# Nineteen more tiles are transposed on VectorE in blocks of 32 by 32, in a two-block model of 256 tokens

## The chip, the cores and the metric

The kernel runs on one core of one Trainium2 chip, in one launch. The metric is device time in microseconds, the median of several runs. A core has TensorE (PE, matmuls and transposes through the systolic array), VectorE (DVE), ScalarE (ACT), GpSimd (POOL) and SyncE (SP, which here issues the loads of weights). Each engine works through its own queue of instructions strictly in order. Data lie in on-chip buffers of 128 partitions; results of PE go to PSUM banks, from which the other engines read them.

## The reference

A first block on x (256 tokens, 2048 channels): RMS norm, one projection, three kinds of attention (gated linear, forgetting, memory), gates, an output projection, and an MLP with squared ReLU. A second block on its result: RMS norm, a projection, sparse attention beside a pool mixer, a gated sum of the two branches, memory cross-attention, and a SwiGLU. Cut to the lines whose results the change touches:

```python
xn = rms_norm(h, attn_norm_g)
gq, gk, gv, gg, ga, fq, fk, fv, fg, ff, mq, mg = split(xn @ w_in)
fq_h, fk_h = rms_norm(heads(fq), g1), rms_norm(heads(fk), g2)   # normed streams, as mk and mq
o = rms_norm(concat([gla_o, fox_o, mem_o]), out_norm_g)
gate = concat([silu(gg), sigmoid(fg), sigmoid(mg)])
h = h + (o * gate) @ w_out
u = relu(rms_norm(h, mlp_norm_g) @ w_up)
h = h + (u * u) @ w_down
# block 2, x = h
z = rms_norm(x, ln_mix_pre) @ w_in_2
a, p = nsa_attention(...), pool_mixer(...)
y = (g_a * (a @ w_br_attn) + g_p * (p @ w_br_pool)) @ w_mix_out
```

All of it is float32.

## The kernel before

**Matmuls.** Every product with a weight matrix is a group: 512 output columns for 256 tokens, summed over 16 k-tiles of 128 rows (8 for the groups called dn, ba and bp). To keep float32 accuracy with PE's faster type, both factors are split in a high and a low part. For each k-tile and each half of the tokens PE runs three matmuls of 128 by 512: high by high (line 460), high by weight-low (461), low by weight-high (462). A group of 16 k-tiles has 96 of them, one of 8 k-tiles has 48.

**Weights.** They arrive by DMA in units of two k-tiles (512 KB) into five raw buffers. For each unit ACT copies out the high part `wh` (line 133, called from `split`) and DVE subtracts to get the low part `wl` (line 366). There are six pairs of `wh` and `wl`, and up to four units are split ahead of the one that PE works on.

**Activations.** The factor that is not a weight must stand transposed, channels on partitions. A tile is 256 tokens by 512 channels: eight squares of 128 by 128, and four k-tiles once it is transposed, that is 24 matmuls of a group. There are two ways. `T_group` (under `T_split` and `T_plain`) transposes on PE against an identity: two quads of four squares, each into a PSUM bank (line 203), from which ACT writes the high part and DVE the low part. `T_dve` transposes on DVE: 16 instructions (line 525) that each turn eight blocks of 32 by 32, from buffer to buffer; then ACT and DVE split as before. Before the change `T_dve` serves the 16 u tiles of the MLP and 11 tiles of the SwiGLU, 27 tiles with 432 such instructions; all other tiles go over PE.

**Order.** The order of the instructions on each engine is fixed when the kernel is built. `run_groups` writes the matmuls of all groups in order. What has to be done with a group's result (scales, norms, gates, transposes) is a task, a generator that yields between small steps. `pump` runs between k-tiles and puts steps of waiting tasks into the queues as long as counters of estimated time (`pe_t`, `act_t`, `dve_t`) stay within LIM of each other; `dv` prices a DVE instruction. When a group's matmuls come to a k-tile whose transposed tile has no finished task yet, `need` calls `finish`, which writes the steps of all waiting tasks at once, ahead of the next matmul. SP issues the loads in the order of the units.

**Names.** The groups follow each other as mk, mv, gq, gk, sm, gv0, gv1, mq, fq, fk, fv, gg0, gg1, fg, mg, out0 to out3, up and dn in turn (dn7_0 to dn7_3 are the last four of the MLP), kvc and q0 and others of block 2's projection, m0 to m7, bp0 to bp3, ba0 to ba3, mix0 to mix3, xk, xv, xo, fg0.0 and so on. dn7_c adds into the stream x at columns c, and `norm_T` of it makes the transposed tile c that kvc needs first (16 k-tiles, tile 0 for k-tiles 0 to 3, up to tile 3). ba_c completes the branch sum y of columns c in `br`, which mix0 needs in the same manner. In the orders, s and a number are activation buffers, gb the banks of groups, pb the banks of transposes and attention, vecs the norms' gains.

Of the kernel before, what the change touches and what calls it, by code (L numbers as in the profile page):

```python
# [10 lines left out]
F32 = mybir.dt.float32  # L11
# [3 lines left out]
OP = mybir.AluOpType  # L15
# [93 lines left out]
class Program:  # L109
# [405 lines left out]

        yield from self.T_group(nat, sink)

    def T_dve(self, f, hi, lo):

        (g,) = yield from self.F.wait()  # L520
        x = f.rearrange("p (t k q j) -> p k t q j", t=2, k=4, q=4)
        y = g.rearrange("p (k t a i) -> p k t a i", k=4, t=2, a=4)
        for a in range(4):
            for q in range(4):
                self.nc.vector.transpose(y[32 * q:32 * q + 32, :, :, a], x[32 * a:32 * a + 32, :, :, q])  # L525
                self.dv(256)
                if q % 2:
                    yield 1
        self.F.put(f)
        self.act(hi, g)  # L530
        yield 1
        self.tt(lo, g, hi.bitcast(F32), OP.subtract)
        self.F.put(g)

    def T_plain(self, nat, dst, gain=None):
# [69 lines left out]
def v3(f, a):  # L605
    return f.rearrange("p (a b) -> p a b", a=a)


class Kernel(Program):
# [57 lines left out]
    def headnorm_T(self, banks, key, gain, name):  # L667
        yield from self.until(("rs", key))
        rs = self.rs[key]
        f, j = yield from self.F.wait(2)  # L670
        for t in range(2):
            self.scopy(v3(f, 2)[:, t], banks[t], rs[:, t:t + 1])
        yield "B"
        self.act(j, f, AF.Square)
        yield 1
        ss = self.stat(8)
        self.red(ss, v3(j, 8), OP.add)
        self.F.put(j)
        r = self.rstd(ss, 8, 128.0)
        yield 1  # L680
        self.tt(v3(f, 8), v3(f, 8), r[:, :, None].to_broadcast([128, 8, 128]), OP.mult)
        yield 1
        (o,) = yield from self.F.wait()
        yield from self.T_plain(v3(f, 2), o, gain)
        self.F.put(f)
        self.S[name] = o
        self.ev.add(name)

    def plain_T(self, banks, key, scale, name, keep=False):
        yield from self.until(("rs", key))  # L690
        rs = self.rs[key]
        if scale != 1.0:
            r2 = self.stat(2)
            self.ts(r2, rs, scale)
            rs = r2
        f, o = yield from self.F.wait(2)
        for t in range(2):
            self.scopy(v3(f, 2)[:, t], banks[t], rs[:, t:t + 1])
        yield "B"
        yield from self.T_plain(v3(f, 2), o)  # L700
        if keep:
            self.S["nat", name] = f
        else:
            self.F.put(f)
        self.S[name] = o
        self.ev.add(name)
# [316 lines left out]
    def gate(self, banks, grp, silu):  # L1023
        rs = self.rs["x"]
        (s,) = yield from self.F.wait()
        s3 = v3(s, 2)
        for t in range(2):
            self.act(s3[:, t], banks[t], AF.Sigmoid, scale=rs[:, t:t + 1])
            if silu:
                self.stt(s3[:, t], banks[t], rs[:, t:t + 1], s3[:, t], OP.mult, OP.mult)  # L1030
        if grp == 3:
            self.free_TT("x")
        yield "B"
        yield from self.until(("o", grp))
        o = self.S.pop(("o", grp))
        self.tt(o, o, s, OP.mult)
        self.F.put(s)
        yield 1
        h, l = yield from self.R.wait(2)
        yield from self.T_split(v3(o, 2), self.vec("out_norm_g", 4 * grp, 4), h, l)  # L1040
        self.F.put(o)
        self.TT["o"][0][grp], self.TT["o"][1][grp] = h, l
        self.ev.add(("oT", grp))

# [4 lines left out]
    def norm_T(self, f, c, key, gain, sq):  # L1049

        f3 = v3(f, 2)
        self.sq_into(f3, sq, c)
        self.nsq[key] = self.nsq.get(key, 0) + 1
        if self.nsq[key] == 4:
            self.fin_ssq(sq, key)
        yield 1
        h, l = yield from self.R.wait(2)
        yield from self.T_split(f3, self.vec(gain, 4 * c, 4), h, l)
        H, L = self.TT.setdefault(key, ([None] * 4, [None] * 4))
        H[c], L[c] = h, l  # L1060
        self.ev.add((key, c))
# [392 lines left out]

    def a_T(self, f, x):
        h, l = yield from self.R.wait(2)
        yield from self.T_split(v3(f, 2), None, h, l)
        self.F.put(f)
        self.TT["a"][0].append(h)
        self.TT["a"][1].append(l)  # L1460
        self.ev.add(("a", x))
# [72 lines left out]
    def br(self, banks, i, c):  # L1534

        m = 4 * i + c
        yield from self.until(("m", m))
        s = self.S["m", m]
        s3 = v3(s, 2)
        self.act(s, s, AF.Sigmoid)  # L1540
        for t in range(2):
            self.tt(s3[:, t], banks[t], s3[:, t], OP.mult)
        if c == 3:
            self.free_TT("p" if i else "a")
        yield "B"
        if i == 1:
            self.ev.add(("yp", c))
            return
        y = self.S.pop(("m", c))
        p = self.S.pop(("m", 4 + c))  # L1550
        self.tt(y, y, p, OP.add)
        self.F.put(p)
        yield 1
        h, l = yield from self.R.wait(2)
        yield from self.T_split(v3(y, 2), None, h, l)
        self.F.put(y)
        H, L = self.TT.setdefault("y", ([None] * 4, [None] * 4))
        H[c], L[c] = h, l
        self.ev.add(("y", c))
# [599 lines left out]
```

## Time and profile before

| | |
|---|---|
| median of three runs | 2617.18 us (2617.09 to 2617.91) |
| the profiled execution | 2616.85 us, of which the span is 2615.1 us |
| mean granted clock of PE | 0.998 |
| PE busy | 2591.0 us, 99% of the span |
| DVE busy | 1670.6 us, 64% |
| ACT busy | 1264.2 us, 48% |
| DVE instructions of block transposes | 432 |
| PE matmuls on line 203, transposes among them | 484 |

The span is from the first to the last instruction on the chip; the run's own time is 1.75 us longer. An engine that is busy for nearly the whole span, with the chain of waits running along it, sets the time. The other engines matter where it waits for them. Start times in the profile place the groups: out1 begins at 404.4 us, up2 at 516.9, dn7_2 at 1151.1, dn7_3 at 1162.9, kvc at 1174.7, ba3 at 1669.4, mix0 at 1681.2, mix1 at 1703.9.

### The profile page before, as it was taken

What the parts mean: (1) busy time and instruction counts of PE and PEld (TensorE: products, weight loads), DVE (VectorE), ACT (ScalarE), POOL (GpSimd) and SP (SyncE); (2) the same over time, 40 slices, a digit from 0 to 9 for tenths busy, and PEclk for the clock granted to TensorE, in tenths of its full rate; (3) what the DMA queues carried; (4) which work ended last, traced back from release to release, by engine and by line L of the source; (5) the groups of instructions that cost most, each with busy time, mean ns of one, the idle gap of its engine ahead of it and who ended that gap; (6) DMA issues with size and microseconds to landing.
All of it is one profiled execution on the core that took longest, in us unless ns stands there. A gap on an engine that the chain in (4) does not pass through costs nothing.

```text
span 2615.1 us, 31982 instructions
## 1 busy us (share of the span) xinstructions
PE 2591.0 (99%) x11980; PEld 2148.5 (82%) x11980; DVE 1670.6 (64%) x2310; ACT 1264.2 (48%) x1697; POOL 76.6 (3%) x97
## 2 busy tenths in 40 slices
PE   9999999999999999999999999999999999999998
PEld 7888888888888888888888888888788888888886
DVE  6567655686677567755566445666766656565656
ACT  7544544544444444444465444465554444444443
POOL 0001000000000000001000000000000000000001
PEclk9999999999999999999999999999999999999999
DMA  9543465555566556565444557555455555555653
GB/s 346 206 138 121 156 222 186 185 193 195 193 204 229 193 194 233 190 209 195 152 139 150 190 177 258 203 197 188 139 186 191 197 190 199 189 198 188 215 188 129
DMA packets 138892, 500.19 MB, mean 191 GB/s; under 512 B 15649, under 2 KB 16593, under 8 KB 138736
## 3 DMA queue, kind: packets, MB, share of 16 engines
q1 hardware_dynamic: 131760, 473.16, 53.4%
q0 software_dynamic: 6976, 24.98, 2.8%
q8 instruction: 94, 1.54, 0.2%
q14 instruction: 62, 0.51, 0.1%
HBM read 493.33 MB, written 7.88 MB: 192 GB/s over the span
## 4 chain that ended last, share of the span: by engine, by line
PE 94%; issue 4%; DVE 1%; ACT 0%; DMA 0%; POOL 0%; SPq 0%; DVEq 0%; ACTq 0%; POOLq 0%
PE gb L460 29%; PE gb L462 29%; PE gb L461 29%; PE pb L197 4%; PE pb L203 2%; DVE s L169 0%; DVE wl L366 0%; DMA s<-memT 0%; DVE s L158 0%; ACT wh L133 0%; POOL st L232 0%; PE gb L450 0%; ACT s L133 0%; PE gb L452 0%; PE gb L451 0%
## 5 line engine op out<-in xcount | busy, mean ns | idle before, releaser
L366 DVE TENSOR_TENSOR wl<-raw,wh 128x1024 fp32r<-128x1024 f32 (+1 forms) x876 | 1057.8, 1219 | 572.2 <-ACT wh L133 565.5
L460 PE MATMUL gb<-wh,s 128*128 128x512 f32 x3496 | 1380.0, 395 | 2.0 <-ACT wh L133 1.8
L461 PE MATMUL gb<-wl,s 128*128 128x512 f32 x3496 | 1363.3, 390 | 2.5 <-DVE wl L366 2.5
L462 PE MATMUL gb<-wh,s 128*128 128x512 f32 x3496 | 1363.6, 390 | 0.3 <-DVE s L169 0.3
L133 ACT ACTIVATE wh<-raw 128x1024 fp32r<-128x1024 f32 (+1 forms) x878 | 916.3, 1055 | 809.2 <-PE gb L462 765.1
L460 PEld LDWEIGHTS gb<-wh,s 128*128 128x128 f32 x3496 | 657.5, 188 | 138.4 <-ACT wh L133 3.4
L462 PEld LDWEIGHTS gb<-wh,s 128*128 128x128 f32 x3496 | 656.9, 188 | 138.8 <-DVE s L169 1.0
L461 PEld LDWEIGHTS gb<-wl,s 128*128 128x128 f32 x3496 | 657.7, 188 | 136.3 <-DVE wl L366 3.8
L525 DVE STREAM_TRANSPOSE s<-s 32x256 f32<-32x256 f32 x432 | 188.2, 436 | 7.8
L158 DVE TENSOR_TENSOR s<-gb,s 128x512 f32<-128x512 f32 x144 | 97.6, 690 | 124.6 <-PE gb L462 94.5
L133 ACT ACTIVATE s<-gb,st 128x512 f32<-128x512 f32 (+1 forms) x112 | 70.0, 642 | 177.4 <-PE gb L462 166.0
L133 ACT ACTIVATE s<-s 128x1024 fp32r<-128x1024 f32 (+3 forms) x89 | 82.5, 928 | 90.0 <-DVE s L525 68.5
L197 PE MATMUL pb<-s,s 128*128 128x128 f32 (+4 forms) x720 | 116.5, 301 | 1.3 <-DVE s L158 0.9
L197 PEld LDWEIGHTS pb<-s,s 128*128 128x128 f32 x720 | 97.7, 191 | 9.5 <-DVE s L158 1.3
L133 ACT ACTIVATE s<-pb 128x512 f32<-128x512 f32 (+4 forms) x117 | 56.9, 506 | 73.9 <-PE pb L203 49.7
L203 PE MATMUL pb<-cc,s 128*128 128x128 f32 (+1 forms) x484 | 73.2, 274 | 5.6 <-DVE s L169 5.6
L203 PEld LDWEIGHTS pb<-cc,s 128*128 128x128 f32 (+1 forms) x484 | 59.7, 141 | 22.4 <-DVE s L169 6.9
L158 DVE TENSOR_TENSOR s<-s,s 128x60 f32<-128x60 f32 (+5 forms) x123 | 73.8, 633 | 0.6
L133 ACT ACTIVATE s<-pb,vecs 128x256 fp32r<-128x256 f32 (+2 forms) x109 | 42.2, 453 | 50.0 <-PE pb L203 40.5
L163 DVE TENSOR_SCALAR s<-gb,st 128x512 f32<-128x512 f32 (+1 forms) x32 | 20.9, 658 | 67.8 <-PE gb L462 51.5
L169 DVE SCALAR_TENSOR_TENSOR s<-pb,vecs,s 128x256 fp32r<-128x256 f32 (+1 forms) x104 | 40.0, 435 | 29.0 <-ACT s L133 29.0
L133 ACT ACTIVATE s<-s,st 128x128 f32<-128x128 f32 (+2 forms) x73 | 32.8, 450 | 31.7 <-DVE st L163 30.4
(113 smaller groups left out, 550.7 us busy)
## 6 DMA issues: line engine op xcount, KB each, us to landing
raw<-w_in SPq DMA_DIRECT2D x216, 512.0 KB, 4.2
raw<-w_up SPq DMA_DIRECT2D x216, 512.0 KB, 4.4
raw<-w_down SPq DMA_DIRECT2D x216, 512.0 KB, 4.6
raw<-w_gate SPq DMA_DIRECT2D x88, 512.0 KB, 4.7
raw<-w_out SPq DMA_DIRECT2D x32, 512.0 KB, 4.5
raw<-w_mix_out SPq DMA_DIRECT2D x32, 512.0 KB, 4.7
raw<-w_br_pool SPq DMA_DIRECT2D x16, 512.0 KB, 5.2
raw<-w_br_attn SPq DMA_DIRECT2D x16, 512.0 KB, 4.5
```

The source lines that it names most:

```text
L133: self.nc.scalar.activation(out, in_, func, **kw)
L158: self.nc.vector.tensor_tensor(out, a, b, op)
L163: self.nc.vector.tensor_scalar(out, a, s1, None, op0=op0)
L169: self.nc.vector.scalar_tensor_tensor(out, a, s, b, op0, op1)
L197: self.nc.tensor.matmul(out, lhsT, rhs, start=start, stop=stop)
L203: self.nc.tensor.transpose(out, in_, self.ident[:k, :k])
L366: self.nc.vector.tensor_sub(l[:, :m], r, h[:, :m].bitcast(F32))
L460: mm(o, H[:, c:c + 128], wh, start=st, stop=False)
L461: mm(o, H[:, c:c + 128], wl, start=False, stop=False)
L462: mm(o, L[:, c:c + 128], wh, start=False, stop=sp)
L525: self.nc.vector.transpose(y[32 * q:32 * q + 32, :, :, a], x[32 * a:32 * a + 32, :, :, q])
```

## The change

Nineteen tiles that went over PE go through DVE's block transpose: the normed keys and queries mk, mq, fq, fk (`headnorm_T`), gq and gk (`plain_T` with `keep`), three of the four gated outputs (`gate`), columns 0 to 2 of the streams after attention and after the MLP (`norm_T` with key h and h2, three each), the first half of the sparse attention's result (`a_T`), and columns 0 to 2 of the branch sum (`br`). The sixteen instructions are taken out of `T_dve` into `T_blocks`; `T_dve` can apply a gain while splitting, and keep its source. The high and low parts are then made from the transposed tile in a buffer instead of from PSUM banks.

```diff
--- before.py
+++ after.py
@@ -515,9 +515,8 @@
 
         yield from self.T_group(nat, sink)
 
-    def T_dve(self, f, hi, lo):
-
-        (g,) = yield from self.F.wait()
+    def T_blocks(self, f, g):
+
         x = f.rearrange("p (t k q j) -> p k t q j", t=2, k=4, q=4)
         y = g.rearrange("p (k t a i) -> p k t a i", k=4, t=2, a=4)
         for a in range(4):
@@ -526,10 +525,19 @@
                 self.dv(256)
                 if q % 2:
                     yield 1
-        self.F.put(f)
-        self.act(hi, g)
-        yield 1
-        self.tt(lo, g, hi.bitcast(F32), OP.subtract)
+
+    def T_dve(self, f, hi, lo, gain=None, keep=False):
+        (g,) = yield from self.F.wait()
+        yield from self.T_blocks(f, g)
+        if not keep:
+            self.F.put(f)
+        if gain is None:
+            self.act(hi, g)
+            yield 1
+            self.tt(lo, g, hi.bitcast(F32), OP.subtract)
+        else:
+            self.split_T(v3(g, 4), gain, v3(hi, 4), v3(lo, 4))
+            yield 1
         self.F.put(g)
 
     def T_plain(self, nat, dst, gain=None):
@@ -681,8 +689,9 @@
         self.tt(v3(f, 8), v3(f, 8), r[:, :, None].to_broadcast([128, 8, 128]), OP.mult)
         yield 1
         (o,) = yield from self.F.wait()
-        yield from self.T_plain(v3(f, 2), o, gain)
+        yield from self.T_blocks(f, o)
         self.F.put(f)
+        self.scopy(o, o, gain)
         self.S[name] = o
         self.ev.add(name)
 
@@ -697,7 +706,10 @@
         for t in range(2):
             self.scopy(v3(f, 2)[:, t], banks[t], rs[:, t:t + 1])
         yield "B"
-        yield from self.T_plain(v3(f, 2), o)
+        if keep:
+            yield from self.T_blocks(f, o)
+        else:
+            yield from self.T_plain(v3(f, 2), o)
         if keep:
             self.S["nat", name] = f
         else:
@@ -1037,8 +1049,11 @@
         self.F.put(s)
         yield 1
         h, l = yield from self.R.wait(2)
-        yield from self.T_split(v3(o, 2), self.vec("out_norm_g", 4 * grp, 4), h, l)
-        self.F.put(o)
+        if grp < 3:
+            yield from self.T_dve(o, h, l, self.vec("out_norm_g", 4 * grp, 4))
+        else:
+            yield from self.T_split(v3(o, 2), self.vec("out_norm_g", 4 * grp, 4), h, l)
+            self.F.put(o)
         self.TT["o"][0][grp], self.TT["o"][1][grp] = h, l
         self.ev.add(("oT", grp))
 
@@ -1055,7 +1070,10 @@
             self.fin_ssq(sq, key)
         yield 1
         h, l = yield from self.R.wait(2)
-        yield from self.T_split(f3, self.vec(gain, 4 * c, 4), h, l)
+        if key != "hx" and c < 3:
+            yield from self.T_dve(f, h, l, self.vec(gain, 4 * c, 4), True)
+        else:
+            yield from self.T_split(f3, self.vec(gain, 4 * c, 4), h, l)
         H, L = self.TT.setdefault(key, ([None] * 4, [None] * 4))
         H[c], L[c] = h, l
         self.ev.add((key, c))
@@ -1454,8 +1472,11 @@
 
     def a_T(self, f, x):
         h, l = yield from self.R.wait(2)
-        yield from self.T_split(v3(f, 2), None, h, l)
-        self.F.put(f)
+        if x == 0:
+            yield from self.T_dve(f, h, l)
+        else:
+            yield from self.T_split(v3(f, 2), None, h, l)
+            self.F.put(f)
         self.TT["a"][0].append(h)
         self.TT["a"][1].append(l)
         self.ev.add(("a", x))
@@ -1552,8 +1573,11 @@
         self.F.put(p)
         yield 1
         h, l = yield from self.R.wait(2)
-        yield from self.T_split(v3(y, 2), None, h, l)
-        self.F.put(y)
+        if c < 3:
+            yield from self.T_dve(y, h, l)
+        else:
+            yield from self.T_split(v3(y, 2), None, h, l)
+            self.F.put(y)
         H, L = self.TT.setdefault("y", ([None] * 4, [None] * 4))
         H[c], L[c] = h, l
         self.ev.add(("y", c))
```

The order of the queues changes with it, since `T_blocks` yields eight times a tile, and since the tasks' estimated times differ. Three places follow.

PE where kvc begins, before. The tile s23 with its low part s15 is transposed tile 0; s27 is the stream's columns 3, and wh2 is the second unit of kvc:

```order
L460 MATMUL gb2_84<-wh2_74,s23_186_7449 128x512
L461 MATMUL gb2_84<-wl2_75,s23_186_7449 128x512
L462 MATMUL gb2_84<-wh2_74,s15_187_7450 128x512
L460 MATMUL gb3_85<-wh2_74,s23_186_7449 128x512
L461 MATMUL gb3_85<-wl2_75,s23_186_7449 128x512
L462 MATMUL gb3_85<-wh2_74,s15_187_7450 128x512
L203 MATMUL pb0_86<-cc_92,s27_104_2695 128x128 x4
L460 MATMUL gb2_84<-wh3_76,s11_188_7544 128x512
L461 MATMUL gb2_84<-wl3_77,s11_188_7544 128x512
L462 MATMUL gb2_84<-wh3_76,s30_189_7545 128x512
```

PE in the same place now, from the end of dn7_3. Here s5 and s10 are the high and low part of tile 0, s24 the stream's columns 3:

```order
L460 MATMUL gb1_83<-wh0_70,s16_183_7200 128x512
L461 MATMUL gb1_83<-wl0_71,s16_183_7200 128x512
L462 MATMUL gb1_83<-wh0_70,s8_184_7201 128x512
L203 MATMUL pb0_86<-cc_92,s24_107_2754 128x128 x4
L460 MATMUL gb2_84<-wh1_72,s5_192_7543 128x512
L461 MATMUL gb2_84<-wl1_73,s5_192_7543 128x512
L462 MATMUL gb2_84<-wh1_72,s10_193_7544 128x512
L460 MATMUL gb3_85<-wh1_72,s5_192_7543 128x512
L461 MATMUL gb3_85<-wl1_73,s5_192_7543 128x512
L462 MATMUL gb3_85<-wh1_72,s10_193_7544 128x512
L203 MATMUL pb1_87<-cc_92,s24_107_2754 128x128 x4
```

The first quad of tile 3 stood behind the 24 matmuls of tile 0; it now stands ahead of the first one, and that quad needs the last sum of dn7_3.

DVE from the sum of dn7_2 (s18) to that of dn7_3 (s27), before:

```order
L158 TENSOR_TENSOR s18_103_2693<-gb2_84,s18_103_2693 128x512
L158 TENSOR_TENSOR s18_103_2693<-gb3_85,s18_103_2693 128x512
L366 TENSOR_TENSOR wl1_73<-raw3_68,wh1_72 128x1024
L366 TENSOR_TENSOR wl2_75<-raw4_69,wh2_74 128x1024
L169 SCALAR_TENSOR_TENSOR s10_191_7622<-pb3_89,vecs_91,s14_190_7621 128x256 x2
L366 TENSOR_TENSOR wl3_77<-raw0_65,wh3_76 128x1024
L169 SCALAR_TENSOR_TENSOR s10_191_7622<-pb2_88,vecs_91,s14_190_7621 128x256 x2
L366 TENSOR_TENSOR wl4_79<-raw1_66,wh4_78 128x1024
L158 TENSOR_TENSOR s27_104_2695<-gb0_82,s27_104_2695 128x512
L158 TENSOR_TENSOR s27_104_2695<-gb1_83,s27_104_2695 128x512
```

DVE in the last part of the same stretch now; s21 is the stream's columns 2, and s27, s12 and s15 are tiles 0, 1 and 2 while they are being transposed. Of the sixteen transposes since the sum of dn7_2 (s21), the first four stand ahead of these rows:

```order
L366 TENSOR_TENSOR wl1_73<-raw3_68,wh1_72 128x1024
L366 TENSOR_TENSOR wl2_75<-raw4_69,wh2_74 128x1024
L524 STREAM_TRANSPOSE s15_200_7703<-s21_106_2752 32x8x32 x2
L524 STREAM_TRANSPOSE s12_197_7632<-s19_105_2750 32x8x32 x2
L524 STREAM_TRANSPOSE s27_194_7545<-s3_104_2748 32x8x32 x2
L366 TENSOR_TENSOR wl3_77<-raw0_65,wh3_76 128x1024
L524 STREAM_TRANSPOSE s15_200_7703<-s21_106_2752 32x8x32 x2
L524 STREAM_TRANSPOSE s12_197_7632<-s19_105_2750 32x8x32 x2
L366 TENSOR_TENSOR wl4_79<-raw1_66,wh4_78 128x1024
L524 STREAM_TRANSPOSE s27_194_7545<-s3_104_2748 32x8x32 x2
L158 TENSOR_TENSOR s24_107_2754<-gb0_82,s24_107_2754 128x512
L158 TENSOR_TENSOR s24_107_2754<-gb1_83,s24_107_2754 128x512
```

Between the two sums stood four weight splits and four instructions of a quarter of a tile each; there are four weight splits and sixteen block transposes now.

DVE from the sum of ba2 (s21) to the rows that follow on ba3, before; s7 is the tile of columns 3:

```order
L158 TENSOR_TENSOR s21_250_10426<-gb2_84,s21_250_10426 128x512
L158 TENSOR_TENSOR s21_250_10426<-gb3_85,s21_250_10426 128x512
L366 TENSOR_TENSOR wl4_79<-raw1_66,wh4_78 128x1024
L158 TENSOR_TENSOR s21_250_10426<-s21_250_10426,s19_233_9479 128x1024
L366 TENSOR_TENSOR wl5_81<-raw2_67,wh5_80 128x1024
L366 TENSOR_TENSOR wl0_71<-raw3_68,wh0_70 128x1024
L158 TENSOR_TENSOR s12_258_11057<-pb2_88,s27_257_11056 128x512
L158 TENSOR_TENSOR s12_258_11057<-pb3_89,s27_257_11056 128x512
L366 TENSOR_TENSOR wl1_73<-raw4_69,wh1_72 128x1024
```

DVE in that place now, up to the finished sum of columns 3 (s19). The sum of ba2 was s31, and s23, s21 and s5 are tiles 0, 1 and 2 of y on their way:

```order
L524 STREAM_TRANSPOSE s21_269_11119<-s26_259_10432 32x8x32 x2
L524 STREAM_TRANSPOSE s23_266_11033<-s20_258_10309 32x8x32 x2
L366 TENSOR_TENSOR wl0_71<-raw3_68,wh0_70 128x1024
L524 STREAM_TRANSPOSE s5_272_11204<-s31_260_10555 32x8x32 x2
L366 TENSOR_TENSOR wl1_73<-raw4_69,wh1_72 128x1024
L524 STREAM_TRANSPOSE s21_269_11119<-s26_259_10432 32x8x32 x2
L158 TENSOR_TENSOR s19_261_10678<-gb0_82,s19_261_10678 128x512
L158 TENSOR_TENSOR s19_261_10678<-gb1_83,s19_261_10678 128x512
L366 TENSOR_TENSOR wl2_75<-raw0_65,wh2_74 128x1024
L158 TENSOR_TENSOR s19_261_10678<-s19_261_10678,s16_246_9868 128x1024
L524 STREAM_TRANSPOSE s5_272_11204<-s31_260_10555 32x8x32 x2
L524 STREAM_TRANSPOSE s21_269_11119<-s26_259_10432 32x8x32 x2
```

Twelve block transposes and five weight splits stand between the products of ba2 and the finished sum of columns 3; of tile 0's low part nothing is made yet at the end of these rows.

## Rows read from the trace of the kernel before

**Rows 1.** The page: busy time by engine, the clock, the chain by engine.
```profile
PE 2591.0 (99%) x11980; PEld 2148.5 (82%) x11980; DVE 1670.6 (64%) x2310; ACT 1264.2 (48%) x1697; POOL 76.6 (3%) x97
PEclk9999999999999999999999999999999999999999
PE 94%; issue 4%; DVE 1%; ACT 0%; DMA 0%; POOL 0%; SPq 0%; DVEq 0%; ACTq 0%; POOLq 0%
```

**Rows 2.** Timeline of PE in out1: start us, duration us, engine, line, names, count.
```profile
408.23 0.39 PE L462 MATMUL gb<-wh,s 128*128 128x512 f32 x1
408.46 0.60 PE L203 MATMUL pb<-cc,s 128*128 128x128 f32 x4
408.81 0.48 PE L460 MATMUL gb<-wh,s 128*128 128x512 f32 x1
409.13 0.40 PE L461 MATMUL gb<-wl,s 128*128 128x512 f32 x1
```

**Rows 3.** Busy time by stretch: us, PE, PEld, DVE, ACT, POOL, PEclk, DMA share, GB/s.
```profile
404.40:427.10 22.70, 22.70 (x106) 18.82 (x105) 12.66 (x15) 11.28 (x16) 0.00 (x0) 1.00 0.57 182
516.90:538.70 21.80, 21.80 (x98) 18.04 (x97) 17.74 (x25) 11.46 (x13) 0.00 (x0) 1.00 0.58 194
...
1162.90:1174.70 11.80, 11.80 (x58) 9.78 (x57) 7.73 (x11) 7.04 (x12) 0.53 (x1) 1.00 0.74 237
1174.70:1197.40 22.70, 22.70 (x106) 18.81 (x105) 12.50 (x16) 10.64 (x16) 4.28 (x6) 1.00 0.89 313
...
1669.40:1681.20 11.80, 11.80 (x57) 9.80 (x56) 8.43 (x10) 6.16 (x7) 0.00 (x0) 1.00 0.53 179
1681.20:1703.90 22.70, 22.70 (x105) 18.81 (x105) 9.21 (x10) 5.66 (x7) 2.10 (x4) 1.00 0.66 231
1703.90:1727.70 23.80, 22.38 (x98) 17.95 (x97) 20.47 (x29) 18.56 (x32) 0.00 (x0) 1.00 0.66 221
224.90:258.70 33.80, 33.80 (x199) 29.65 (x198) 28.00 (x48) 13.28 (x22) 3.27 (x2) 1.00 0.33 110
```

**Rows 4.** Costliest groups of the page: busy us, mean ns of one, idle before.
```profile
L133 ACT ACTIVATE wh<-raw 128x1024 fp32r<-128x1024 f32 (+1 forms) x878 | 916.3, 1055 | 809.2 <-PE gb L462 765.1
...
L525 DVE STREAM_TRANSPOSE s<-s 32x256 f32<-32x256 f32 x432 | 188.2, 436 | 7.8
...
L203 PE MATMUL pb<-cc,s 128*128 128x128 f32 (+1 forms) x484 | 73.2, 274 | 5.6 <-DVE s L169 5.6
```

**Rows 5.** Timeline of DVE in up1, where a u tile is transposed.
```profile
509.31 1.22 DVE L366 TENSOR_TENSOR wl<-raw,wh 128x1024 fp32r<-128x1024 f32 x1
510.56 1.80 DVE L525 STREAM_TRANSPOSE s<-s 32x256 f32<-32x256 f32 x4
512.39 1.23 DVE L366 TENSOR_TENSOR wl<-raw,wh 128x1024 fp32r<-128x1024 f32 x1
513.53 1.22 DVE L158 TENSOR_TENSOR s<-s,s 128x1024 fp32r<-128x1024 f32 x1
```

**Rows 6.** Timeline of DVE around dn7_3 and kvc.
```profile
1170.56 0.87 DVE L169 SCALAR_TENSOR_TENSOR s<-pb,vecs,s 128x256 fp32r<-128x256 f32 x2
...
1174.21 1.37 DVE L158 TENSOR_TENSOR s<-gb,s 128x512 f32<-128x512 f32 x2 [1.65 <-PE gb L462]
```

**Rows 7.** Timeline of DVE around ba3, mix0 and mix1.
```profile
1669.01 1.30 DVE L158 TENSOR_TENSOR s<-gb,s 128x512 f32<-128x512 f32 x2 [0.70 <-ACT wh L133]
1670.23 1.22 DVE L366 TENSOR_TENSOR wl<-raw,wh 128x1024 fp32r<-128x1024 f32 x1
...
1704.18 1.43 DVE L158 TENSOR_TENSOR s<-gb,s 128x512 f32<-128x512 f32 x2 [11.09 <-ACT junk L133]
```

**Rows 8.** Timeline of PE in fg0.0, at an idle time of 4.43 us.
```profile
1887.53 1.46 PE L203 MATMUL pb<-cc,s 128*128 128x128 f32 x8 [4.43 <-DVE s L169]
...
1891.56 0.41 PE L462 MATMUL gb<-wh,s 128*128 128x512 f32 x1
```

**Rows 9.** Busy time by stretch, the 5 us around the end of that idle time.
```profile
1887.00:1892.00 5.00, 4.18 (x16) 3.09 (x17) 5.00 (x12) 2.17 (x8) 1.60 (x1) 0.66 0.44 168
```


## The prediction

> **What bounds the kernel now.** I read the page's busy times first, then the chain, then the stretches group by group, and last the queues of single engines. TensorE is busy for 99% of the span, its clock stays at the full level in all forty slices, and 94% of the chain runs along it [rows 1]. So time is saved only by what is taken off TensorE's queue, and lost only by what makes it wait. VectorE has 36% of the span free on average [rows 1], but the average hides how it is spread. In the groups of 16 k-tiles between which u tiles are transposed, VectorE works 17.74 of 21.80 us; in fk, beside attention, 28.00 of 33.80; in dn7_3 7.73 of 11.80 and in ba3 8.43 of 11.80 [rows 3]. The last two are the short groups: there the next matrix, which needs the fresh tiles, begins after half the time.
>
> **What leaves TensorE.** Nineteen tiles of two quads are 38 quads, 152 transposes of 128 by 128. In out1 a quad stands between two matmuls: the next matmul starts 0.35 us after the quad did, and the one behind it 0.32 us later instead of the usual 0.23, which is the distance from the matmul ahead to the quad [rows 2]. A quad thus costs 0.35 + 0.09 = 0.44 us, and 38 cost 16.7 us. A second view agrees: out1, with one tile's transposes, lasts 22.70 us, up2 without any 21.80 [rows 3]; 19 times 0.90 is 17.1. I take 16.7.
>
> **What comes to VectorE.** Nineteen times 16 is 304 block transposes of 0.44 us [rows 4], 0.45 with the gap behind each, against some 16 copies and subtractions that go: about 132 us in all, so 1.80 ms or 69% of the span. One tile takes 16 × 0.45 = 7.2 us of VectorE for 0.88 us of TensorE.
>
> Here a rule of the Trainium skill can be set beside the rows. The trace has 0.44 us for four squares on TensorE [rows 2], and for eight squares 16 block transposes of 0.44 us, 7.0 us [rows 4]. The page "VectorE: DVE Perf Modes" (The three transpose paths) gives 390 ns on TensorE and 311 ns on VectorE for one square of bf16, in 32 by 32 blocks only, and its rules for kernel authors say to transpose 128 by 128 on TensorE where a result in PSUM will do. By its figures a tile would cost VectorE about 2.5 us (an estimate: 8 × 311 ns), and the stalls below would largely vanish, which is the second case below; the trace has nearly three times that. Its advice, TensorE, speaks against this change.
>
> **Where VectorE has the room.** In long groups a tile that becomes free is needed a whole group later. mk to fk, the gated outputs and the h tiles fall into out0 to up0 and before: 12 to 18 us of other work in 21.8 [rows 3] plus 7.2 us of transposes at most once a group. I count 19 to 20 of 21.8 us in out1 to up0; in gk and fk up to 2 us more than the group has, which four units of weights split ahead (10.9 us of matmuls) absorb. I take 0 there, with 0 to 4 us as bounds. The reloaded branch tile (one more goes to DRAM and back) lies on queues that wait for nothing near; ACT, at 48% [rows 1], takes a few more table loads beside TensorE; both are taken as nothing.
>
> **Where it has not: dn7_3 to kvc.** I walk the new queue from the end of dn7_2's last matmul, with durations from the rows: a weight split 1.14 us, or 1.25 ahead of a transpose; four transposes 1.83; a sum of two halves 1.22 (1.33 ahead of a transpose); a tile-wide subtraction 1.14; a low part of a quarter tile 0.44 [rows 5 to 7]. On VectorE: sum of dn7_2 1.3, sixteen transposes 7.2, four weight splits 4.9, sum of dn7_3 1.3: done at 14.7 us. TensorE has dn7_3's 48 matmuls, 48 × 0.227 = 10.9 us, and then, in the new order, a quad of columns 3 ahead of kvc's first matmul. It waits 14.75 − 10.9 = 3.9 us. (Before, VectorE was idle for 1.65 us ahead of this sum, waiting for TensorE [rows 6].) Next, the first low part of tile 0 stands behind a weight split, two small reductions and four transposes: 14.75 + 1.1 + 0.4 + 1.8 + 0.45 = 18.5; TensorE comes at 15.6 and waits 3.0. Tile 0's 24 matmuls and the second quad end at 24.0. Before the first low part of tile 1 VectorE still does three low parts of tile 0, four of tile 3, twelve transposes and two weight splits: 1.3 + 1.75 + 5.4 + 2.3, and 0.45 for that part itself: 11.2 us, at 29.7. TensorE comes at 24.5 and waits 5.2. Tile 2's first low part is there at 34.6, TensorE comes at 35.1. In all 12.0 us. The stretch has 34 block transposes, 15.3 us: VectorE has 39.3 us of work in 33.5 us of matmuls.
>
> **ba3 to mix0** works the same way. Between the products of ba2 and the finished sum of columns 3 stand sum 1.3, twelve transposes 5.4, five weight splits 6.0, and sums and products of 3.6: it is done at 16.4 us, TensorE comes for its quad at 10.9 and waits 5.5. Behind it come eight transposes and the subtraction for tile 0's low part (3.7 + 1.2): 21.25, against 17.3 for TensorE, 3.95. Tile 0 ends at 26.7. Tile 1's last transpose is at 29.6, its high part, a copy of 1.05 us on ACT [rows 4], at 30.65: 3.95. Its low part is at 34.25, against 31.1: 3.15. Tile 2's low part stands behind a weight split whose pair of buffers TensorE frees late, at 41.85, against 39.7: 2.15. In all 18.7 us; VectorE has 42.5 us of work in 33.5.
>
> **Clock and mix1.** After an idle time of 4.43 us in fg0.0 the next eight transposes take 1.46 us instead of twice 0.6, and the granted clock is 0.66 over those 5 us, so for a while the lower level, 1.2 GHz [rows 2, 8, 9]: 0.34 × 5.0 = 1.7 us of matmul time. Each stretch above has such waits; the first slow spell hides in the wait after it, the last does not: 2 × 1.7 = 3.4 us, with 0 and 7 as bounds. In the other direction, mix1 has 2.0 us more than a group of its kind: ACT's squares of mix0's result stood ahead of the weight copies, and VectorE was idle for 11.09 us [rows 3, 7]. In the new order three more units are split ahead of them, so that goes: −2.0.
>
> **Sum.** From the profiled execution, 2616.85 us (0.33 below the median): −16.7 + 12.0 + 18.7 + 3.4 − 2.0 = +15.4, 2632.2. I predict 2632 us.
>
> **The rivals.** *Two shorter stalls, or one:* the walk charges every wait in full; if one stretch stalls as worked out and the other for a third, 2616.85 − 16.7 − 2.0 + 12 + 6 + 1 to 3 is 2617 to 2619. For it: the tasks were priced to fit. Against: rows and order leave no slack in the sums of 14.7 and 16.4 us. *The blocks are absorbed:* VectorE has 944 us free and receives 132, and transposes u tiles in up2 with no idle time on TensorE (21.80 busy of 21.80) [rows 1, 3]. Then −16.7 and −2.0 plus a few us of waits: 2598 to 2608, faster. The mechanism would be a block transpose that costs much less between weight splits than in the rows; the point is at dn7_3, where the sixteen would have to fit in 10.9 − 7.5 = 3.4 us, 0.21 us each. The rows with four in 1.83 us [rows 5] speak against it. *Attention stalls too:* fk has 5.8 us free on VectorE [rows 3] and receives a tile of 7.2 less the copies it loses; the same near mq, fq and m6. With 2 to 4 us there and the clock at the lower level more often, 2640 to 2650.
>
> **How the numbers follow.** Forecast, both stretches stall (2623 to 2640): 0.66. Shorter stalls (2612 to 2622): 0.14. Absorbed (2598 to 2611): 0.11. Attention too (above 2640): 0.09. A measurement of this kernel tells 0.2%, 5.2 us, from no change, so faster is below 2612, slower above 2622.4: 0.11, 0.14 and 0.75. The range takes in most of the second and part of the fourth: 2614 to 2643.
>
> **What would show it.** Right: line 203 has 332 instructions instead of 484, the block transposes number 736 at 0.44 us; out1 to out3 last 21.8 us; TensorE has waits released by VectorE of 4, 3 and 5 us from kvc's first quad on, and of 5.5, 4, 4, 3 and 2 in mix0, and a granted clock below 1 in both; kvc ends 12 us and mix0 19 us later against the groups ahead; mix1 is 21.8 long. Wrong: no wait above 2 us at either place, or waits of that size in mq to fk or in m0 to m7, or a block transpose of less than 0.3 us.

## The result, and the profile after

The changed kernel takes 2637.38 us (median of 4 runs, 2636.42 to 2638.48) against 2617.55 us for the kernel before (4 runs, 2617.09 to 2619.88): a ratio of 1.0073, with a 95% interval of 1.0062 to 1.0085. It is 20 us slower; 2632 us had been predicted, 15 us slower, in a range of 2614 to 2643.

The page of the changed kernel, busy times, clock, chain by engine, and the two groups of transposes:

```profile
PE 2588.6 (98%) x11828; PEld 2142.0 (81%) x11828; DVE 1795.6 (68%) x2602; ACT 1269.7 (48%) x1695; POOL 79.5 (3%) x99
PEclk9999999999999999989999999899999999999999
PE 91%; issue 5%; DVE 3%; DMA 1%; ACT 0%; POOL 0%; SPq 0%; DVEq 0%; ACTq 0%; POOLq 0%
...
L524 DVE STREAM_TRANSPOSE s<-s 32x256 f32<-32x256 f32 x736 | 320.7, 436 | 13.7 <-ACT s L133 0.5
...
L203 PE MATMUL pb<-cc,s 128*128 128x128 f32 (+1 forms) x332 | 53.4, 285 | 14.4 <-DVE s L158 9.1
```

Against [rows 1] and [rows 4] VectorE has 125 us more to do and 304 block transposes more, at the same 436 ns each; line 203 lost 152 instructions, 19.8 us of TensorE's busy time. The digits of TensorE's clock have two 8s (slices below 90% of full speed), where there were only 9s, and the chain now spends 3% on VectorE.

Busy times by stretch (us; PE, PEld, DVE, ACT and POOL busy; granted clock; DMA share; GB/s), for dn7_3, kvc, ba3, mix0, mix1 and out1 of the changed kernel:

```profile
1150.90:1167.90 17.00, 12.35 (x54) 9.52 (x52) 16.55 (x29) 7.41 (x14) 0.00 (x0) 0.96 0.51 173
1167.90:1200.10 32.20, 27.61 (x100) 21.44 (x101) 22.99 (x41) 13.58 (x23) 5.87 (x9) 0.81 0.75 261
1669.30:1686.00 16.70, 11.81 (x54) 9.60 (x52) 16.33 (x25) 6.14 (x6) 0.00 (x0) 0.98 0.52 177
1686.00:1726.90 40.90, 30.25 (x103) 23.05 (x102) 25.45 (x41) 13.98 (x21) 2.11 (x4) 0.76 0.42 147
1726.90:1748.70 21.80, 21.80 (x98) 18.08 (x97) 14.00 (x18) 12.87 (x22) 0.00 (x0) 1.00 0.59 188
396.90:418.60 21.70, 21.70 (x97) 18.00 (x96) 19.40 (x31) 11.44 (x16) 0.00 (x0) 1.00 0.54 184
```

In [rows 3] the same six were 11.80, 22.70, 11.80, 22.70, 23.80 and 22.70 us long. out1 loses its 0.9 us (0.94 by the start times of the groups, 22.70 and 21.76 us), mix1 its 2.0. The first two grow by 14.7 us together, ba3 and mix0 by 23.1. VectorE is busy for 39.5 of 49.2 and 41.8 of 57.6 us there. The groups ahead of dn7_3 are 11.9 us shorter together, those between the two places 2.8.

TensorE's waits at kvc's start and then at mix0's start in the changed kernel (start, duration, line, names, count, in brackets the idle time ahead and what ended it):

```profile
1165.89 0.33 PE L203 MATMUL pb<-cc,s 128*128 128x128 f32 x1 [3.91 <-DVE s L158]
...
1167.86 0.79 PE L460 MATMUL gb<-wh,s 128*128 128x512 f32 x1 [0.47 <-ACT s L133]
...
1170.22 0.80 PE L462 MATMUL gb<-wh,s 128*128 128x512 f32 x1 [1.15 <-DVE s L169]
...
1178.50 0.50 PE L460 MATMUL gb<-wh,s 128*128 128x512 f32 x1 [1.11 <-ACT s L133]
...
1181.57 0.80 PE L462 MATMUL gb<-wh,s 128*128 128x512 f32 x1 [2.33 <-DVE s L169]
...
1685.23 1.08 PE L203 MATMUL pb<-cc,s 128*128 128x128 f32 x4 [4.89 <-DVE s L158]
...
1690.09 0.80 PE L462 MATMUL gb<-wh,s 128*128 128x512 f32 x1 [2.93 <-DVE s L158]
...
1700.96 0.51 PE L460 MATMUL gb<-wh,s 128*128 128x512 f32 x1 [2.57 <-ACT s L133]
...
1704.66 0.80 PE L462 MATMUL gb<-wh,s 128*128 128x512 f32 x1 [2.97 <-DVE s L158]
...
1714.69 0.50 PE L462 MATMUL gb<-wh,s 128*128 128x512 f32 x1 [2.19 <-DVE s L158]
```

The first of each list is the quad of columns 3 that stands ahead of the first matmul. Line 462 needs the low part, line 460 the high part of the next tile. Each wait is released by VectorE, or by ACT right behind it. The quad's place itself matters little by these rows: behind it TensorE waits for tile 0's low part anyway, until 1170.22 and 1690.09.

VectorE's queue at the places that the prediction timed, first dn7_3 and kvc, then ba3 and mix0:

```profile
1151.78 1.28 DVE L158 TENSOR_TENSOR s<-gb,s 128x512 f32<-128x512 f32 x2
...
1165.14 1.29 DVE L158 TENSOR_TENSOR s<-gb,s 128x512 f32<-128x512 f32 x2
...
1169.68 1.67 DVE L169 SCALAR_TENSOR_TENSOR s<-s,vecs,s 128x256 fp32r<-128x256 f32 x4
...
1181.03 1.67 DVE L169 SCALAR_TENSOR_TENSOR s<-s,vecs,s 128x256 fp32r<-128x256 f32 x4
...
1187.33 1.23 DVE L366 TENSOR_TENSOR wl<-raw,wh 128x1024 fp32r<-128x1024 f32 x1 [2.45 <-ACT wh L133]
...
1668.89 1.30 DVE L158 TENSOR_TENSOR s<-gb,s 128x512 f32<-128x512 f32 x2
...
1683.95 1.22 DVE L158 TENSOR_TENSOR s<-s,s 128x1024 f32<-128x1024 f32 x1
...
1688.81 1.23 DVE L158 TENSOR_TENSOR s<-s,s 128x1024 fp32r<-128x1024 f32 x1
...
1696.76 1.23 DVE L366 TENSOR_TENSOR wl<-raw,wh 128x1024 fp32r<-128x1024 f32 x1 [1.49 <-ACT wh L133]
...
1703.38 1.23 DVE L158 TENSOR_TENSOR s<-s,s 128x1024 fp32r<-128x1024 f32 x1
...
1710.47 1.23 DVE L366 TENSOR_TENSOR wl<-raw,wh 128x1024 fp32r<-128x1024 f32 x1 [4.73 <-ACT wh L133]
...
1713.42 1.22 DVE L158 TENSOR_TENSOR s<-s,s 128x1024 fp32r<-128x1024 f32 x1
```

From the sum of dn7_2 (start at 1151.78), that of dn7_3 ends 14.65 us later, the first low part of tile 0 18.3, of tile 1 29.7 us later; 14.7, 18.5 and 29.7 were worked out. From the sum of ba2 (start at 1668.89), the finished columns 3 come 16.3 us later (walked: 16.4) and the low part of tile 0 21.15 (21.25), but that of tile 1 35.7 (34.25) and of tile 2 45.75 (41.85). In between VectorE has idle times that ACT's weight copies end: 2.45 us in kvc, behind which no wait of TensorE follows, and 1.49 and 4.73 in mix0. The walk had such a late copy only ahead of tile 2, and a shorter one. A copy waits until TensorE is done with the pair of buffers, and TensorE was slow: in five microseconds of mix0 the changed kernel's stretch reads

```profile
1690.00:1695.00 5.00, 4.91 (x14) 3.94 (x15) 4.89 (x10) 0.60 (x1) 0.53 (x1) 0.50 0.08 13
```

with a granted clock of 0.50, the lower level of 1.2 GHz.

### The profile page after: what moved, and what is told of

Same layout as the page of the kernel before. It is cut to its first block, busy times and chain, and to the rows that moved or that the text cites. A ratio compares the mean times of both kernels' runs of the same rounds, so it can differ in the third digit from the quotient of the medians.

```text
span 2636.7 us, 31964 instructions
## 1 busy us (share of the span) xinstructions
PE 2588.6 (98%) x11828; PEld 2142.0 (81%) x11828; DVE 1795.6 (68%) x2602; ACT 1269.7 (48%) x1695; POOL 79.5 (3%) x99
## 4 chain that ended last, share of the span: by engine, by line
PE 91%; issue 5%; DVE 3%; DMA 1%; ACT 0%; POOL 0%; SPq 0%; DVEq 0%; ACTq 0%; POOLq 0%
PE gb L460 28%; PE gb L462 28%; PE gb L461 28%; PE pb L197 4%; DVE s L524 1%; PE pb L203 1%; DVE wl L366 1%; DVE s L158 1%; DVE s L169 1%; DMA s<-memT 0%; DMA raw<-w_down 0%; ACT wh L133 0%; POOL st L232 0%; PE gb L450 0%; PE gb L452 0%
## 5 line engine op out<-in xcount | busy, mean ns | idle before, releaser
L524 DVE STREAM_TRANSPOSE s<-s 32x256 f32<-32x256 f32 x736 | 320.7, 436 | 13.7 <-ACT s L133 0.5
L133 ACT ACTIVATE s<-pb 128x512 f32<-128x512 f32 (+4 forms) x107 | 51.3, 499 | 71.1 <-PE pb L203 47.7
L158 DVE TENSOR_TENSOR s<-s,s 128x1024 fp32r<-128x1024 f32 (+5 forms) x127 | 78.6, 651 | 0.7
L203 PE MATMUL pb<-cc,s 128*128 128x128 f32 (+1 forms) x332 | 53.4, 285 | 14.4 <-DVE s L158 9.1
L203 PEld LDWEIGHTS pb<-cc,s 128*128 128x128 f32 (+1 forms) x332 | 42.9, 147 | 27.9 <-DVE s L158 10.5
L163 DVE TENSOR_SCALAR s<-gb,st 128x512 f32<-128x512 f32 (+1 forms) x28 | 17.9, 645 | 53.2 <-PE gb L462 37.0
L232 POOL TENSOR_TENSOR st<-st,nhalf 128x8 f32<-128x8 f32 (+2 forms) x21 | 27.9, 1331 | 799.9 <-DVE st L165 799.9
L133 ACT ACTIVATE s<-s,vecs 128x256 fp32r<-128x256 f32 (+1 forms) x87 | 39.5, 519 | 16.9 <-DVE s L524 13.0
```

Of the source, the lines that this page charges most:

```text
L133: self.nc.scalar.activation(out, in_, func, **kw)
L158: self.nc.vector.tensor_tensor(out, a, b, op)
L163: self.nc.vector.tensor_scalar(out, a, s1, None, op0=op0)
L203: self.nc.tensor.transpose(out, in_, self.ident[:k, :k])
L232: self.nc.gpsimd.tensor_tensor(r, t, self.nhalf[:, :k], op=OP.pow)
```

## The experiments

Each edit is against the changed kernel.

**Six tiles back (both_back).**

```diff
-        if key != "hx" and c < 3:
+        if key != "hx" and c < (3 if key == "h" else 0):
...
-        if c < 3:
+        if c < 0:
```

> The six tiles at the two short-group boundaries (columns 0 to 2 of the stream after the MLP, and of the branch sum) go over TensorE again; the other 13 new tiles stay on VectorE. Theory: the loss sits in these two places alone, so from the changed kernel the 14.6 us by which dn7_3 and kvc grew (less 1.6 gained in dn7_1 and dn7_2), the 23.0 us of ba3 and mix0 (less 1.9 gained in ba1 and ba2) and the 2.0 us gained at mix1 are taken back: 2637.4 - 13.0 - 19.2 = 2605, faster than before by 12. Rival (a fuller VectorE costs time in many places): the gain of 13 tiles is lost elsewhere, 2615 or more.

Measured: 2605.64 us (2604.89 to 2606.99), 0.9954 of the kernel before (0.9939 to 0.9969). dn7_3, kvc, ba3 and mix0 of this kernel:

```profile
1152.30:1164.10 11.80, 11.80 (x58) 9.78 (x56) 7.73 (x11) 7.04 (x12) 0.53 (x1) 1.00 0.76 232
1164.10:1186.80 22.70, 22.70 (x106) 18.81 (x104) 12.51 (x16) 10.65 (x16) 4.28 (x6) 1.00 0.88 315
1657.90:1669.70 11.80, 11.80 (x58) 9.78 (x56) 8.43 (x10) 6.16 (x7) 0.00 (x0) 1.00 0.53 179
1669.70:1692.40 22.70, 22.70 (x106) 18.81 (x104) 9.17 (x10) 5.70 (x7) 2.10 (x4) 1.00 0.66 230
```

They are as long as before, with VectorE's busy times of before. The other 13 tiles give 12 us: 13 times 0.94, the difference by which out1 and its like are shorter. So the loss sits in the two places, and a fuller VectorE costs nothing elsewhere. This kernel is faster than both.

**One place at a time (h2_back, y_back).** The same edit, at the first line alone and at the second alone.

> Only the three tiles of the stream after the MLP go over TensorE again; the branch sum stays on VectorE. Theory (two separate places that add up): 2637.4 - 13.0 = 2624, and mix0 still takes 41 us and ba3 17. Rival (one delay that carries on from kvc to mix0): mix0 becomes shorter too, and the time falls to 2615 or less.

> Only the three tiles of the branch sum go over TensorE again; the stream after the MLP stays on VectorE. Theory: 2637.4 - 19.2 = 2618, kvc still 32 us long, mix0 22.7. Rival (the loss is in VectorE's total load): about a sixth of the loss goes with a sixth of the tiles, 2632 to 2635.

Measured: 2624.2 us (2623.38 to 2626.38) and 2618.11 us (2616.52 to 2618.87). The two places add up, and neither feeds the other by more than a microsecond: with the branch sum on VectorE and the stream not, mix0 is 40.2 us long (40.9 in the changed kernel); with the stream on VectorE and the branch sum not, kvc is 31.3 (32.2).

**Busy waits (warm).** At ten places of TensorE's queue, where it waits in kvc and mix0, 116 matmuls are put in whose results nobody uses, so that it does not stand idle; the core of the edit:

```diff
+    def fill(self, n, own=False):
+        w = self.pair[0]
+        b = self.gbk[0] if own else self.banks[0]
+        for _ in range(n):
...
+            self.nc.tensor.matmul(b["ap"], w[:, :128], w[:, :512], start=True, stop=True)
...
+            if un.kt0 % 4 == 0:
+                self.fill(FILL.get((g.name, un.kt0 // 4, "H"), 0))
```

> The changed kernel with 116 matmuls more on TensorE (a weight tile times itself into a free bank, results unused) in the ten places of kvc and mix0 where it waits, 3.4 us ahead of the first quad in kvc and less than each wait by the walk elsewhere; the queues of the other engines are the same. It asks for the part of the two stretches that is not the walk's waits (39.5 us lost in the trace, 30.7 walked). Theory: that part is matmuls at the lower clock level, which busy waits prevent; granted clock near 1 in both stretches, and 2637.4 - 8 = 2629 (2627 to 2631). Rival: VectorE sets the pace there, and what the clock costs is hidden: 2636 to 2638. Other rival: the added matmuls come late and delay the real ones: 2640 or more.

Measured: 2629.71 us (2628.33 to 2630.52). dn7_3 with kvc, and ba3 with mix0, of this kernel:

```profile
1150.90:1197.50 46.60, 45.41 (x200) 36.05 (x199) 39.22 (x70) 21.06 (x36) 5.87 (x9) 1.00 0.72 240
1666.60:1718.90 52.30, 50.75 (x223) 40.55 (x222) 41.69 (x65) 20.07 (x26) 2.10 (x4) 1.00 0.52 172
```

The clock is 1.00 in both. They last 46.6 and 52.3 us instead of 49.2 and 57.6. Without waits they would last 33.6 (an estimate: the 34.5 us of before, less 0.94 for the transposes that left), so 13.0 and 18.7 us are waits; the walk had 12.0 and 18.7. The rest, 2.6 + 5.3 = 7.9 us of the changed kernel's loss, was the clock; the medians differ by 7.7. In the changed kernel itself TensorE is busy for 40.0 and 42.1 us there, 14.9 more than twice 33.6: about 7 of these slow microseconds hid in the waits, which are shorter than walked.

With the clock held up VectorE keeps the walk's times in mix0 too. The sum of ba2 and the low parts of tiles 1 and 2 in this kernel, where line 163 is what was line 158:

```profile
1666.18 1.30 DVE L163 TENSOR_TENSOR s<-gb,s 128x512 f32<-128x512 f32 x2
...
1699.13 1.22 DVE L163 TENSOR_TENSOR s<-s,s 128x1024 fp32r<-128x1024 f32 x1
...
1707.11 1.22 DVE L163 TENSOR_TENSOR s<-s,s 128x1024 fp32r<-128x1024 f32 x1
```

These low parts are finished 34.2 and 42.15 us after the start of that sum (walked: 34.25 and 41.85; in the changed kernel 35.7 and 45.75).

**Half the transposes (half_tr).**

```diff
+        if rows < 4:
+            self.nc.gpsimd.memset(y[:, :, :, rows:], 0.0)
...
-                self.nc.vector.transpose(y[32 * q:32 * q + 32, :, :, a], x[32 * a:32 * a + 32, :, :, q])
+                if a < rows:
+                    self.nc.vector.transpose(y[32 * q:32 * q + 32, :, :, a], x[32 * a:32 * a + 32, :, :, q])
```

> The changed kernel with 8 of the 16 block transposes left out at the six tiles of the two places (the other half of those tiles is zero); the queues are otherwise the same, so quads and low parts stand where they stood. Theory (VectorE's amount of work sets the waits): 3.6 us less per tile; the walk gives 5.7 us of waits at kvc instead of 12.0 and 11.5 at mix0 instead of 18.7, and less time at the low clock: 2637.4 - 13.5 - 2 to 6 = 2618 to 2622. Rival (the order is the cause: a quad and low parts put ahead of ready matmuls): 2632 or more.

Measured: 2618.61 us (2616.48 to 2619.49). TensorE's waits in mix0 of this kernel:

```profile
1674.25 0.66 PE L203 MATMUL pb<-cc,s 128*128 128x128 f32 x4 [3.08 <-DVE s L158]
...
1677.32 0.80 PE L462 MATMUL gb<-wh,s 128*128 128x512 f32 x1 [1.96 <-DVE s L158]
...
1686.50 0.50 PE L460 MATMUL gb<-wh,s 128*128 128x512 f32 x1 [0.71 <-ACT s L133]
...
1687.93 0.50 PE L462 MATMUL gb<-wh,s 128*128 128x512 f32 x1 [0.70 <-DVE s L158]
...
1695.90 0.50 PE L462 MATMUL gb<-wh,s 128*128 128x512 f32 x1 [2.23 <-DVE s L158]
```

The quad still stands ahead of the first matmul, and still waits, but dn7_3 to kvc lost 10.9 us and ba3 to mix0 9.6 against the changed kernel. They are now 4.6 and 14.3 us over 33.6, for walked waits of 5.7 and 11.5 and some clock. In a given order the amount of work on VectorE sets the waits; the order of TensorE's queue alone would have left them. What another order on VectorE's own queue would save with the same work, say all blocks of tile 0 ahead of those of tiles 1 and 2, was not tried: VectorE is busy for 39.5 and 41.8 us of the two stretches in the changed kernel, only 5.9 and 8.2 more than 33.6.

**Weight splits on GpSimd (pool_wl).**

```diff
-            self.nc.vector.tensor_sub(l[:, :m], r, h[:, :m].bitcast(F32))
+            eng = self.nc.gpsimd if un.grp.name in ("kvc", "mix0") else self.nc.vector
+            eng.tensor_sub(l[:, :m], r, h[:, :m].bitcast(F32))
```

> The changed kernel with the low parts of the 16 weight units of kvc and mix0 subtracted on GpSimd instead of VectorE, queues otherwise the same; the transposes stay. Theory (VectorE's amount of work, whatever it is made of): some 5 to 6 us less on VectorE ahead of each first quad; walked waits 6 at kvc and 12.7 at mix0, and with less time at the low clock 2637.4 - 12 - 0 to 4 = 2621 to 2626. Rival (the transposes themselves are the limit, by their order): 2634 to 2638. Other rival: GpSimd needs more than the 2.72 us per unit that TensorE takes, and TensorE waits for it: over 2640.

Measured: 2632.76 us (2630.91 to 2635.03), between what the theory and its first rival gave, so a miss for both. dn7_3 and ba3 fell by 3.7 and 2.9 us, as VectorE came earlier to the quads; kvc stayed at 32.0 us and mix0 grew to 42.9. VectorE's queue and GpSimd's in this kernel:

```profile
1151.67 2.29 DVE L367 TENSOR_TENSOR wl<-raw,wh 128x1024 fp32r<-128x1024 f32 x1
...
1155.19 7.18 DVE L525 STREAM_TRANSPOSE s<-s 32x256 f32<-32x256 f32 x16
1162.40 1.29 DVE L158 TENSOR_TENSOR s<-gb,s 128x512 f32<-128x512 f32 x2
...
1164.89 1.71 DVE L165 TENSOR_SCALAR st<-st 128x2 f32<-128x2 f32 x1
...
1176.33 2.71 DVE L525 STREAM_TRANSPOSE s<-s 32x256 f32<-32x256 f32 x6
1179.07 4.89 DVE L169 SCALAR_TENSOR_TENSOR s<-s,vecs,s 128x256 fp32r<-128x256 f32 x4
```

```profile
1150.48 2.39 POOL L367 TENSOR_TENSOR wl<-raw,wh 128x1024 fp32r<-128x1024 f32 x1 [118.41 <-ACT wh L133]
1157.16 9.41 POOL L367 TENSOR_TENSOR wl<-raw,wh 128x1024 fp32r<-128x1024 f32 x4 [4.29 <-ACT wh L133]
...
1177.40 2.40 POOL L367 TENSOR_TENSOR wl<-raw,wh 128x1024 fp32r<-128x1024 f32 x1 [7.05 <-ACT wh L133]
...
1180.87 2.41 POOL L367 TENSOR_TENSOR wl<-raw,wh 128x1024 fp32r<-128x1024 f32 x1
```

Four low parts that took 1.67 us in the changed kernel take 4.89 here: two subtractions of GpSimd, from 1177.40 and from 1180.87, fall into them. The DMA issues of GpSimd between them are not the cause: in the changed kernel four low parts take their 1.67 us beside such issues. A weight split beside one takes 2.29 instead of 1.22. Sixteen block transposes in a row, most of them beside four subtractions, take 7.18, 0.45 each as ever, and the sum out of a PSUM bank 1.29. The low parts and the splits have two operands in the buffers, the transposes and the sum only one. But the scaling of two statistics, with one operand, takes 1.71 us in place of 0.17. The Trainium skill, page "GPSIMD Engine Reference", section 1 (Specifications), says that GpSimd's access to the buffers is contended by VectorE's instructions with two operands there, or in a two-port mode. The rows agree on the first; which mode the scaling ran in no run here shows. So the run took work off VectorE and made what was left there longer, and does not by itself say what the theory asked of it; half_tr does.

**One and two tiles at each place (one_each, two_each).** The edit of both_back, with 1 and with 2 in place of 0.

> As the kernel with all six tiles back on TensorE, but columns 0 of both places on VectorE: their transposes can start two short groups earlier. Theory: two more tiles at 0.88 us, no wait: 2605.6 - 1.8 = 2604 (2603 to 2605). Rival (any tile there delays the next matrix): 2608 or more.

> As the one before, with columns 0 and 1 of both places on VectorE. Between the sum of the second tile and its first matmul lie two short groups and a quarter of a long one, 27 us of matmuls; VectorE has 14.4 us of transposes and some 12 us of weight splits and sums in them. Theory: it just fits, 2605.6 - 3.5 = 2602, with up to 4 us of waits where it does not: 2602 to 2606. Rival: as the three tiles, in proportion, 2620 or more.

Measured: 2605.35 us (2604.1 to 2605.94) and 2624.1 us (2623.31 to 2625.11). One tile each gains nothing that can be told from both_back: dn7_1 and ba1 are 0.94 us shorter, but mix0 is 0.84 longer, with a wait of 0.54 us for a low part. It missed its range of 2603 to 2605 by a little. The second expectation was wrong by 20 us, and its rival, a loss in proportion to the tiles, came out. The stretch of two_each from the sum of dn7_1 on, and the first quad in kvc:

```profile
1141.00:1175.00 34.00, 29.54 (x121) 23.03 (x121) 32.27 (x59) 18.83 (x37) 5.88 (x9) 0.86 0.70 235
```

```profile
1165.57 1.50 PE L203 MATMUL pb<-cc,s 128*128 128x128 f32 x4 [2.58 <-DVE s L158]
```

VectorE is busy for 32.27 of 34 us. Up to the last low part of tile 1, at 1176.3, its queue holds 28 transposes (12.7 us), nine weight splits (10.6), sums and reductions (4.1), and 16 low parts of quarter tiles (6.9): 34.3 us, where the expectation had 26 and left the low parts out. That overfills the 27 us. By the order of the queue the blocks of the two tiles also alternate, so that tile 0 is finished late; what that adds was not tried apart. This count is of dn7_2 to kvc; mix0 is 36.5 us long in this kernel, 13.8 more than before, with one wait of 6.79 us for tile 1's high part, and its queue was not counted.

## Why the prediction was right

**What bounds the kernel** held: TensorE's queue, and waits on it at the two short stretches alone.

**The gain per tile** was 0.94 us in the profile's group lengths, for 0.88 worked out from the quad: 17.9 us for nineteen instead of 16.7. **The room elsewhere**, taken as 0 with bounds of 0 to 4, was 0 to within a microsecond: both_back shows 12 us for 13 tiles.

**dn7_3 to kvc and ba3 to mix0.** The waits of 12.0 and 18.7 us were there to within a microsecond when the clock was held up (13.0 and 18.7), and VectorE's times agreed to 0.2 us up to the first instruction that a late weight copy held back. That they follow the amount of VectorE's work is shown by half_tr; how much of them a better order of that work would save stays open.

**The clock** is the term that was mis-sized: 3.4 us were put down, 7.9 were measured. The step that failed is that "the first slow spell hides in the wait after it, the last does not", at 1.7 us for the last.

In kvc the first half of it held. TensorE came later to the next wait, which became shorter for it, and the first low part of tile 1 was there at 29.7 us in the changed kernel and in warm alike. But the last spell cost 2.5 us: from the matmul that takes this low part to the end of kvc are 18.5 us, and 16.1 in warm.

In mix0 it failed. A slow TensorE also frees its weight pairs late, and VectorE's queue stands behind the split of the next one, so VectorE itself came later: late weight copies held it for 1.49 and 4.73 us, in warm only for 2.67 ahead of tile 2, whose low part came 3.6 us later than in warm. One slow spell followed the other, with a granted clock of 0.76 over the 40.90 us, about half of them at the lower level. The last spell added 1.6 us, as put down. The three amounts, 2.5, 3.6 and 1.6 us, are the 7.7 by which the medians of the changed kernel and of warm differ. The bound of 7 us was passed as well.

**mix1's 2.0 us** went as predicted; y_back, where the branch sum is as before, has them again. A part comes back later: behind mix1 the changed kernel takes 888.1 us to the end, the kernel before 887.4 and y_back 887.2; why, no run shows.

**The sum:** −17.9 for −16.7, +13.0 and +18.7 for +12.0 and +18.7, +7.9 for +3.4, −2.0 as predicted; together +19.7, and the medians differ by 19.8. Such an agreement to 0.1 us is partly luck: the spans of the two profiled executions differ by 21.6 us, with 0.7 of the rest in that last part, 0.5 missing from the gain ahead of dn7_3, and 0.7 in the first group, whose end scatters from 31.9 to 34.6 us in kernels that are the same up to there. The larger gain and the larger waits nearly cancel; most of the 5 us between forecast and result is the clock.

**The rivals.** "Absorbed" is refuted at the two places; elsewhere the blocks were absorbed, though at 0.44 us each and not by becoming cheaper. "Attention stalls too" is refuted by the 13 tiles. "Shorter stalls" needed slack that the queues did not have.

## What to carry to other kernels

A transfer of work to an engine with a third of its time free costs time where that free time is not: walk the receiver's queue, in the new order and with durations from the trace, from the last result that frees the work to the first instruction that needs it. If a wait of a few microseconds on TensorE comes out of it, add the slower matmuls behind it, and what a slower TensorE frees late, before hiding anything in the next wait. And a move can be split: 13 of the 19 tiles gain 12 us, the other six lose 32.

## What had not been expected of the hardware

VectorE's instructions with two buffer operands are held up beside a GpSimd subtraction of 128 by 1024 (four low parts took 4.89 us for 1.67, a weight split 2.29 for 1.22), while block transposes run on unchanged (16 in 7.18 us). And TensorE gains from work whose result nobody uses: 116 matmuls in its waits made the kernel 7.7 us faster.
